# A diffusion layer on one core: neighbourhood attention moved in among the value projection, scores built on 128 rows

## The chip, the core and the metric

The kernel runs on one core of a Trainium2 chip. A core has a matrix engine (PE, whose weight loads are a queue of their own, PEld), a vector engine (DVE), a scalar engine (ACT), a general engine (POOL) and a queue that mostly starts transfers (SP), all with queues of their own that run in order. The metric is the device time of one launch in microseconds (us), as the median of several runs. A profiled execution gives in addition a trace of every instruction.

## The reference

One layer over 256 latent tokens and 256 context tokens of width 2048. All tokens are normalised, modulated and projected by `w_in`. Two branches read the result: a neighbourhood attention with 16 heads of 64, and a gated linear attention (GLA); their outputs are gated, projected and added to the input.

```python
h   = layer_norm(x)   * (1 + scale)   + shift
h_c = layer_norm(ctx) * (1 + scale_c) + shift_c
aq, ak, av, az, bq, bk, bv, bz, bg, mga, mgb = split_cols(h @ w_in)      # and the same of h_c
# attention: each latent query, one softmax over its window of the 4 x 64 grid and all context keys
s   = concat(q * 64**-0.5 @ k_window + bias, q * 64**-0.5 @ k_ctx)
y_a = softmax(s) @ concat(v_window, v_ctx)
y_b = gla(bq, bk, bv, bg, ...)
out = (sigmoid(mga) * ((y_a * silu(az)) @ w_br_a) + sigmoid(mgb) * ((y_b * silu(bz)) @ w_br_b)) @ w_out
x   = layer_norm(2**0.25 * x + gate * out)
```

## The kernel before

The modulated tokens lie transposed in SBUF as a high part `hhi` and a low part `hlo` of reduced-precision floats. A product with a weight block is three matmuls: high by high, low weight by high, high weight by low. Each weight block comes by one SP transfer into a tile `r_...` (pool `raw`, four buffers); ACT casts it to `h_...` and DVE subtracts to get `l_...` (three buffers each).

The program is written as a sequence of stages; a scheduler fixes from it the order of each engine's instructions before the run, and may pull independent work between dependent work.

- Modulation with the key projection of the first seven head pairs (`kp`, copied to `kT`).
- The value projection (`va`): three thirds of 352 columns, in each 8 weight blocks by 4 token tiles by 6 matmuls. At the end of a third the four accumulators are copied to `vs`. The last 32 columns (`lt`, `lp`, `lr`) feed the GLA's gates.
- The attention, one pair of heads `p` after the other (8 pairs). `project_pair(p)` splits the pair's keys into `kn` (high) and `kl` (low), copies the 64 rows of each head into both halves of `kh` by four POOL transfers, and projects the queries (`qp`, 48 matmuls of 256 columns; pair 7 projects its keys, `kp`, too). The queries of head `j` go to `qs`: the high part in the head's 64 rows, the low part in the other 64.
- `attend(p)` takes the 256 queries in two halves `qt`. For both heads there are two matmuls into `s`: `qs` by `kh` over 128 rows (high and low query by high key), and `qs` by `kl` over the head's own 64 rows (high query by low key). DVE adds the bias `rb` and takes the negated maximum `nm`, ACT exponentiates both heads into `pr` and sums into `sm`, DVE inverts `sm` and scales both heads, PE transposes the probabilities in 128x128 blocks (`tp`), ACT copies head 0's to `pt`, DVE head 1's. After both halves the products of values and probabilities follow: 8 calls, each into 64 of the 128 rows of `op`, and a copy to `ya`. Each of these calls is two instructions in the trace, since its operands are full floats.
- `attend(p)` stands behind `project_pair(p + 1)` in the program, so that PE has the next pair's projection to do while a softmax runs. Pair 7's attention runs beside the first GLA projections (`bk`, `bq`).
- The GLA by heads (functions in a list `later` are called at set places in it), the gates and the output projections.

Of the kernel before, what the change touches and what calls it, by code (L numbers as in the profile page):

```python
# [8 lines left out]
F32 = mybir.dt.float32  # L9
F32R = mybir.dt.float32r  # L10
# [6 lines left out]
P = 128  # L17
# [70 lines left out]
def tile_backbone_layer(  # L88
# [251 lines left out]
    for p in range(K0):  # L340
# [3 lines left out]
        else:  # L344
            nc.scalar.copy(dst, kdst[p])

    vs = [k8([P, 2, 1024], f"v{i}") for i in range(2)]
    lr = const.tile([P, 512], F32R, name="lr")
    for g in range(3):
        va = [acc(f"va{g}_{t}") for t in range(4)]  # L350
        for k in range(0, KT, 2):
            wh, wl = load(wav[8 * g + k // 2], 2 * AVW, f"av{g}_{k}")
            project_rows([t[:, :AVW] for t in va], wh, wl, k, AVW, 4)
        n = min(AVW, 1024 - AVW * g)
        for t in range(4):
            dst = vs[t // 2][:, t % 2, AVW * g : AVW * g + n]
            if t % 2:
                nc.vector.tensor_copy(dst, va[t][:, :n])
            else:
                nc.scalar.copy(dst, va[t][:, :n])  # L360
        if g == 2:
# [12 lines left out]
    ya = k8([P, NP, T], "ya")  # L374
    half = [slice(64 * j, 64 * j + 64) for j in range(2)]

    def project_pair(p):
        kT = kTs[p // 4][:, p % 4, :]
        if p >= K0:
            kp = acc(f"kp{p}")  # L380
            project_t(f"ak{p}", kp[:], 512, hhi, hlo)
            nc.scalar.copy(kT, kp[:])
        kn = k2([P, 512], f"kn{p}", F32R)
        kl = k2([P, 512], f"kl{p}", F32R)
        split(kn[:], kl[:], kT)
        kh = k4([P, 2, 512], f"kh{p}", F32R)
        for j in range(2):
            for r in half:
                nc.gpsimd.dma_start(kh[r, j, :], kn[half[j], :])
        qp = acc(f"qp{p}")  # L390
        project_t(f"aq{p}", qp[:, :T], T, xh, xl)
        qs = k2([P, 2, T], f"qs{p}", F32R)
        for j in range(2):
            r, o = half[j], half[1 - j]
            nc.scalar.mul(qs[r, j, :], qp[r, :T], 0.125)
            nc.vector.scalar_tensor_tensor(
                qs[o, j, :], qp[r, :T], 0.125, qs[r, j, :].bitcast(F32), ALU.mult, ALU.subtract
            )
        return qs, kh, kl

    def attend(p, qs, kh, kl):
        rt = stream.tile([P, 1024], F32, tag="raw", name=f"rb{p}", bufs=4)
        nc.sync.dma_start(rt[:, :768], rpb[p])
        rb = rt[:, :768].rearrange("p (j c) -> p j c", j=2)
        pt = k8([P, 2, 4, T], f"pt{p}")
        for qt in range(2):
            s2 = pair(f"s{p}_{qt}")
            for j in range(2):
                q = slice(P * qt, P * qt + P)
                mm(s2[:, j, :], qs[:, j, q], kh[:, j, :], True, False)  # L410
                mm(s2[:, j, :], qs[half[j], j, q], kl[half[j], :], False, True)
            o = P * (1 - qt)
            nc.vector.tensor_tensor(out=s2[:, :, :T], in0=s2[:, :, :T], in1=rb[:, :, o : o + T], op=ALU.add)
            nm = tiny([P, 2], "nm")
            nc.vector.tensor_reduce(nm[:], s2[:], AX.X, ALU.max, negate=True)
            pr = k4([P, 2, 512], f"pr{p}_{qt}")
            sm = tiny([P, 2], "sm")
            for j in range(2):
                nc.scalar.activation(
                    pr[:, j, :], s2[:, j, :], AF.Exp, bias=nm[:, j : j + 1], accum_out=sm[:, j : j + 1]  # L420
                )
            nc.vector.reciprocal(sm[:], sm[:])
            for j in range(2):
                nc.vector.tensor_scalar(pr[:, j, :], pr[:, j, :], sm[:, j : j + 1], None, ALU.mult)
                tp = bank(f"tp{p}_{qt}_{j}")
                for kt in range(4):
                    nc.tensor.transpose(tp[:, P * kt : P * kt + P], pr[:, j, P * kt : P * kt + P], ident[:])
                dst = pt[:, j, :, P * qt : P * qt + P]
                src = tp[:].rearrange("p (k q) -> p k q", k=4)
                if j:  # L430
                    nc.vector.tensor_copy(dst, src)
                else:
                    nc.scalar.copy(dst, src)
        op = bank(f"op{p}")
        for kt in range(4):
            for j in range(2):
                c = 128 * p + 64 * j
                mm(
                    op[64 * j : 64 * j + 64, :T],
                    vs[kt // 2][:, kt % 2, c : c + 64],  # L440
                    pt[:, j, kt, :],
                    kt == 0,
                    kt == 3,
                )
        nc.scalar.copy(ya[:, p, :], op[:, :T])

    ready = project_pair(0)
    for p in range(NP):
        ahead = project_pair(p + 1) if p + 1 < NP else None
        attend(p, *ready)  # L450
        ready = ahead


    cs = const.tile([P, 3, T], F32, name="cs")
# [43 lines left out]
                ALU.mult,  # L498
            )

    later = []

    for h in range(NH):
        zp = pair(f"z{h}")
# [420 lines left out]
```

## Time and profile before

| | us |
|---|---|
| median of 3 runs | 1271.01 (1270.85 to 1273.25) |
| the profiled execution: time / span of its trace | 1274.22 / 1272.5 |
| PE busy in the span | 1236.7 |
| value projection, 139.9 to 232.1 in the trace | 92.2 |
| rest of the attention and first GLA key projections, to the first `bq` at 378.6 | 146.5 |

The span is the trace from its first to its last instruction; the time includes what lies around it. A matmul's bar in the trace overlaps with the next one's, so "PE busy" does not say how fast PE gets on: that is read from the starts of successive matmuls.

### The profile page before, as it was taken

To read this page: it belongs to the slowest core of one execution; us is meant where nothing else is said; L and a number is where in the kernel's file an instruction comes from. 1 tells how busy PE (TensorE), PEld (TensorE's weight loads), DVE (VectorE), ACT (ScalarE), POOL (GpSimd) and SP (SyncE) were. 2 spreads that over 40 slices of the span, in tenths; PEclk is the share of its full clock that TensorE was granted. 3 is DMA by queue.
4 is the path that set the end of the run, shared out by engine and by line. 5 is a ranking of instruction groups with operands and counts; after the bars stand their busy time and mean duration, and the time that the engine had idled before them with its cause. 6 is when DMAs were issued, how large, how long until landed. Compare 5 with 4: busy or idle time off the path is not lost.

```text
span 1272.5 us, 17957 instructions
## 1 busy us (share of the span) xinstructions
PE 1236.7 (97%) x7188; PEld 1053.0 (83%) x7188; DVE 739.7 (58%) x1079; ACT 519.6 (41%) x726; POOL 83.1 (7%) x116
## 2 busy tenths in 40 slices
PE   6999999999999999999999999999999999999994
PEld 4667999976679898898888999998888888888784
DVE  7733322666659457456465477875445554555687
ACT  6333322454445333333342454454444444444341
POOL 1111000110201010010010000000000000000112
PEclk9999999999999999999999999999999999999998
DMA  9997333544524325225234367885656555557651
GB/s 378 417 404 283 90 98 107 156 132 132 146 83 146 125 77 183 85 91 173 95 104 150 113 193 244 281 264 197 198 188 194 190 190 191 191 186 289 206 194 66
DMA packets 61427, 229.94 MB, mean 181 GB/s; under 512 B 7377, under 2 KB 7905, under 8 KB 56225
## 3 DMA queue, kind: packets, MB, share of 16 engines
q1 hardware_dynamic: 53424, 189.83, 45.5%
q0 software_dynamic: 7488, 38.68, 8.1%
q8 instruction: 56, 0.92, 0.3%
q10 hardware_dynamic: 432, 0.30, 0.1%
q14 instruction: 27, 0.21, 0.0%
HBM read 222.49 MB, written 2.10 MB: 176 GB/s over the span
## 4 chain that ended last, share of the span: by engine, by line
PE 85%; DVE 5%; DMA 5%; issue 3%; ACT 1%; POOL 0%; SPq 0%; DVEq 0%; POOLq 0%; ACTq 0%
PE bv L139 14%; PE va L139 7%; PE mgb L139 7%; PE mga L139 7%; PE pb L139 7%; PE bk L139 7%; PE kp L139 6%; PE bz L139 6%; PE qp L139 4%; PE pa L139 3%; PE az L139 3%; PE wo L139 3%; PE gp L139 2%; DMA wm<-in_wmod 2%; PE o L139 2%
## 5 line engine op out<-in xcount | busy, mean ns | idle before, releaser
L139 PE MATMUL bv<-l_bv,hhi 128*128 128x512 f32 x256 | 100.0, 391 | 1.0 <-DVE l_bv L145 1.0
L139 PE MATMUL bv<-h_bv,hhi 128*128 128x512 f32 x256 | 99.7, 389 | 0.0
L139 PE MATMUL bv<-h_bv,hlo 128*128 128x512 f32 x256 | 99.6, 389 | 0.0
L139 PE MATMUL bz<-hhi,l_bz 128*128 128x256 f32 x256 | 72.5, 283 | 1.1 <-DVE l_bz L145 1.1
L139 PE MATMUL bz<-hhi,h_bz 128*128 128x256 f32 x256 | 72.4, 283 | 0.0
L139 PE MATMUL bz<-hlo,h_bz 128*128 128x256 f32 x256 | 72.4, 283 | 0.0
L145 DVE TENSOR_TENSOR l_pb<-r_pb,h_pb 128x1024 fp32r<-128x1024 f32 x32 | 39.2, 1225 | 47.8 <-ACT h_pb L143 47.8
L145 DVE TENSOR_TENSOR l_mgb<-r_mgb,h_mgb 128x1024 fp32r<-128x1024 f32 x32 | 39.2, 1225 | 42.2 <-ACT h_mgb L143 42.2
L139 PE MATMUL va<-h_av,hlo 128*128 128x352 f32 x192 | 62.1, 323 | 0.0
L139 PE MATMUL va<-h_av,hhi 128*128 128x352 f32 x192 | 61.9, 322 | 0.0
L139 PE MATMUL va<-l_av,hhi 128*128 128x352 f32 x192 | 61.7, 322 | 0.0
L145 DVE TENSOR_TENSOR l_mga<-r_mga,h_mga 128x1024 fp32r<-128x1024 f32 x32 | 39.2, 1224 | 35.7 <-ACT h_mga L143 35.6
L482 DVE SCALAR_TENSOR_TENSOR gacc<-wg,sc,gacc 128x1024 f32<-128x1024 f32 x32 | 41.1, 1284 | 30.3 <-DMA wg<-in_wgate 30.3
L139 PEld LDWEIGHTS bv<-l_bv,hhi 128*128 128x128 f32 x256 | 48.1, 188 | 11.7 <-DVE l_bv L145 1.9
L145 DVE TENSOR_TENSOR l_av<-r_av,h_av 128x704 fp32r<-128x704 f32 x24 | 21.4, 892 | 60.4 <-ACT h_av L143 60.4
L139 PEld LDWEIGHTS bv<-h_bv,hlo 128*128 128x128 f32 x256 | 48.1, 188 | 9.9
L139 PEld LDWEIGHTS bv<-h_bv,hhi 128*128 128x128 f32 x256 | 48.1, 188 | 9.8
L143 ACT CAST h_bv<-r_bv 128x1024 fp32r<-128x1024 f32 x32 | 33.5, 1048 | 54.7 <-PE bv L139 49.1
L143 ACT CAST h_mgb<-r_mgb 128x1024 fp32r<-128x1024 f32 x32 | 33.7, 1054 | 53.1 <-PE mgb L139 33.1
L145 DVE TENSOR_TENSOR l_bv<-r_bv,h_bv 128x1024 fp32r<-128x1024 f32 x32 | 39.8, 1251 | 26.2 <-ACT h_bv L143 26.2
L139 PE MATMUL kp<-hhi,h_ak 128*128 128x512 f32 x128 | 52.8, 412 | 0.4 <-ACT hhi L143 0.4
L143 ACT CAST h_mga<-r_mga 128x1024 fp32r<-128x1024 f32 x32 | 33.7, 1054 | 47.1 <-PE mga L139 30.5
(326 smaller groups left out, 3655.0 us busy)
## 6 DMA issues: line engine op xcount, KB each, us to landing
wm<-in_wmod POOLq DMA_DIRECT2D x28, 1024.0 KB, 9.5
r_bv<-in_wst SPq DMA_DIRECT2D x32, 512.0 KB, 3.5
wg<-in_wgate SPq DMA_DIRECT2D x32, 512.0 KB, 4.1
r_bz<-in_wst SPq DMA_DIRECT2D x32, 512.0 KB, 4.5
r_mga<-in_wst SPq DMA_DIRECT2D x32, 512.0 KB, 3.5
r_mgb<-in_wst SPq DMA_DIRECT2D x32, 512.0 KB, 3.5
r_pb<-in_wst SPq DMA_DIRECT2D x32, 512.0 KB, 3.4
r_wo<-in_wst SPq DMA_DIRECT2D x24, 512.0 KB, 4.4
```

What stands on the lines that cost most here:

```text
L139: nc.tensor.matmul(o, a, b, start=start, stop=stop)
L143: nc.scalar.copy(hi, src)
L145: nc.vector.tensor_tensor(out=lo, in0=src, in1=hi.bitcast(F32), op=ALU.subtract)
L482: nc.vector.scalar_tensor_tensor(half, raw[:], sc[:, n // 2, 0:1], half, ALU.mult, ALU.add)
```

## The change

- `value_columns(g)`, one third of the value projection, becomes a function. Four rounds `g` project the pairs 2g and 2g + 1, attend both, and then project a third of the values (in the first three rounds).
- `attend` stops at the transposed probabilities `pt`; the value products are `read_values(p)`. Those of a round's two pairs run in the next round, between its two query projections, once their third of the values is there. Those of pair 6 come at the end of round 3, those of pair 7 are the first entry in `later`.
- Scores on 128 rows: `kh` now holds head `j`'s high keys in 64 rows and its low keys in the other 64; `qh` holds the high queries in both halves, `ql` the low queries in both. Both matmuls of a head contract over 128 rows. The second half of `qh` is one more ACT instruction per head, the second half of `ql` one more POOL transfer per head. (The product of low query and low key, left out before, is now in the sum.)
- Of the two scalings of probabilities in a half, ACT takes head 1's. The value products of head 1 stand ahead of head 0's.

```diff
-        kh = k4([P, 2, 512], f"kh{p}", F32R)
-        for j in range(2):
-            for r in half:
-                nc.gpsimd.dma_start(kh[r, j, :], kn[half[j], :])
...
-            nc.scalar.mul(qs[r, j, :], qp[r, :T], 0.125)
-            nc.vector.scalar_tensor_tensor(
-                qs[o, j, :], qp[r, :T], 0.125, qs[r, j, :].bitcast(F32), ALU.mult, ALU.subtract
-            )
...
-                mm(s2[:, j, :], qs[:, j, q], kh[:, j, :], True, False)
-                mm(s2[:, j, :], qs[half[j], j, q], kl[half[j], :], False, True)
...
-    ready = project_pair(0)
-    for p in range(NP):
-        ahead = project_pair(p + 1) if p + 1 < NP else None
-        attend(p, *ready)
-        ready = ahead
+        for j in range(2):
+            for r, src in zip(half, (kn, kl)):
+                nc.gpsimd.dma_start(kh[r, j, :], src[half[j], :])
...
+            nc.scalar.mul(qh[r, j, :], qp[r, :T], 0.125)
+            nc.vector.scalar_tensor_tensor(
+                ql[r, j, :], qp[r, :T], 0.125, qh[r, j, :].bitcast(F32), ALU.mult, ALU.subtract
+            )
+            nc.scalar.mul(qh[o, j, :], qp[r, :T], 0.125)
+            nc.gpsimd.dma_start(ql[o, j, :], ql[r, j, :])
...
+                mm(s2[:, j, :], qh[:, j, q], kh[:, j, :], True, False)
+                mm(s2[:, j, :], ql[:, j, q], kh[:, j, :], False, True)
...
+                if j:
+                    nc.scalar.mul(pr[:, j, :], pr[:, j, :], sm[:, j : j + 1])
+                else:
+                    nc.vector.tensor_scalar(pr[:, j, :], pr[:, j, :], sm[:, j : j + 1], None, ALU.mult)
...
+    def read_values(p):
+        pt = probs.pop(p)
+        op = bank(f"op{p}")
+        for kt in range(4):
+            for j in (1, 0):
+                c = 128 * p + 64 * j
+                mm(op[64 * j : 64 * j + 64, :T], vs[kt // 2][:, kt % 2, c : c + 64], pt[:, j, kt, :], kt == 0, kt == 3)
+        nc.scalar.copy(ya[:, p, :], op[:, :T])
...
+    for g in range(4):
+        q = k8([P, 2, 2, 2, T], f"q{g}", F32R)
+        pairs[2 * g] = project_pair(2 * g, q)
+        for p in sorted(probs):
+            read_values(p)
+        if g == 3:
+            probs[6] = attend(6, *pairs.pop(6))
+        pairs[2 * g + 1] = project_pair(2 * g + 1, q)
+        for p in sorted(pairs):
+            probs[p] = attend(p, *pairs.pop(p))
+        if g < 3:
+            value_columns(g)
+    read_values(6)
...
-    later = []
+    later = [lambda: read_values(NP - 1)]
```

On PE, the scores of pair 0's second half of queries (`s0_1`) stood before like this, with two of the next pairs' query projections around them; `x4` is a run of four equal rows:

```order
L139 MATMUL qp2_2293<-hhi_89,h_aq2_8_2326 128x256
L139 MATMUL s0_1_2247<-kh0_2071,qs0_2137 128x512
L139 MATMUL s0_1_2247<-kl0_2068,qs0_2137 128x512
L139 MATMUL s0_1_2247<-kh0_2071,qs0_2137 128x512
L427 MATMUL tp0_0_0_2234<-ident_73,pr0_0_2228 128x128 x4
L427 MATMUL tp0_0_1_2241<-ident_73,pr0_0_2228 128x128 x4
L139 MATMUL s0_1_2247<-kl0_2068,qs0_2137 128x512
L139 MATMUL qp2_2293<-hhi_89,l_aq2_8_2327 128x256
L139 MATMUL qp2_2293<-hlo_90,h_aq2_8_2326 128x256
```

Now the same scores stand among the values' first third, and no row reads `kl`. An `x3` here is three of the four score matmuls:

```order
L139 MATMUL va0_0_1566<-h_av0_2_1602,hlo_90 128x352
L139 MATMUL s0_1_1482<-kh0_1300,q0_1295 128x512 x3
L405 MATMUL tp0_0_0_1469<-ident_73,pr0_0_1463 128x128 x4
L139 MATMUL s0_1_1482<-kh0_1300,q0_1295 128x512
L405 MATMUL tp0_0_1_1476<-ident_73,pr0_0_1463 128x128 x4
L139 MATMUL va0_1_1567<-h_av0_2_1602,hhi_89 128x352
```

What moved: the four score matmuls are of one kind, and the work that covers the softmax is `va` instead of `qp`.

The value products of pair 0 (`op0`; `64x256` is the shape written) stood before in two pieces, with eight matmuls of a query projection in between, of which the first and the last are shown:

```order
L139 MATMUL s1_0_2362<-kl1_2143,qs1_2212 128x512
L139 MATMUL op0_2274<-pt0_2219,v0_1291 64x256
L139 MATMUL qp3_2435<-hlo_90,h_aq3_0_2438 128x256
...
L139 MATMUL qp3_2435<-hhi_89,h_aq3_8_2468 128x256
L139 MATMUL op0_2274<-pt0_2219,v0_1291 64x256 x3
L139 MATMUL op0_2274<-pt0_2219,v1_1292 64x256 x4
L139 MATMUL qp3_2435<-hhi_89,l_aq3_8_2469 128x256
```

Now the products of pairs 0 and 1 stand in one piece between two query projections:

```order
L139 MATMUL qp2_1824<-hlo_90,h_aq2_8_1857 128x256
L139 MATMUL op0_1893<-pt0_1454,v0_1292 64x256 x4
L139 MATMUL op0_1893<-pt0_1454,v1_1293 64x256 x4
L139 MATMUL op1_1903<-pt1_1511,v0_1292 64x256 x4
L139 MATMUL op1_1903<-pt1_1511,v1_1293 64x256 x4
L139 MATMUL qp3_1922<-hhi_89,h_aq3_0_1925 128x256
```

What moved: sixteen calls run back to back, and the first of them comes behind `qp2`, after the whole first third of the values.

On POOL there were four transfers per pair, issued together; these are the last two pairs' and what follows them, up to the GLA's tiles `gacc` and `wr`:

```order
L389 DMA kh6_2856<-kn6_2852 64x512 x4
L389 DMA kh7_3060<-kn7_3056 64x512 x4
L475 MEMSET gacc_3278 128x2048
L476 DMA gacc_3278<-in_bgate 1x16x128
L461 DMA wr_3267<-in_wg2 128x1024
```

Now a round has eight for `kh` and four that bring the other half of `ql` (a part of tile `q`; `q3` is round 3's). This is the same place:

```order
L362 DMA kh6_2925<-kn6_2921 64x512
L362 DMA kh6_2925<-kl6_2922 64x512
L362 DMA kh6_2925<-kn6_2921 64x512
L362 DMA kh6_2925<-kl6_2922 64x512
L373 DMA q3_2920<-q3_2920 64x256 x2
L362 DMA kh7_3142<-kn7_3138 64x512 x2
L362 DMA kh7_3142<-kl7_3139 64x512 x2
L373 DMA q3_2920<-q3_2920 64x256 x2
L493 MEMSET gacc_3296 128x2048
L494 DMA gacc_3296<-in_bgate 1x16x128
L479 DMA wr_3285<-in_wg2 128x1024
```

What moved: a pair's scores now wait for two short POOL transfers that can start only behind its query projection. In round 3, on PE, pair 6's scores stand behind the value products of pairs 4 and 5; pair 7's first score matmul stands behind eight rows of `bk00`, the next two behind six more, the last behind eight more.

## Rows read from the trace of the kernel before

**Rows 1.** The page: the span, and from its first part PE's busy time, share of the span and instructions.

```profile
span 1272.5 us, 17957 instructions
PE 1236.7 (97%) x7188; PEld 1053.0 (83%) x7188; DVE 739.7 (58%) x1079; ACT 519.6 (41%) x726; POOL 83.1 (7%) x116
```

**Rows 2.** Busy time by stage: from the first value matmul to the last, and from there to the first `bq`. Columns: stretch and its length, then busy time and instructions of PE, PEld, DVE, ACT and POOL, PE's granted clock as a share of 2.4 GHz, share of the 16 transfer engines, GB/s.

```profile
139.90:232.10 92.20, 92.20 (x578) 92.14 (x576) 25.67 (x34) 22.48 (x32) 0.00 (x0) 1.00 0.35 103
232.10:378.60 146.50, 144.16 (x853) 109.24 (x852) 98.08 (x157) 68.99 (x136) 17.11 (x31) 0.99 0.46 134
```

**Rows 3.** PE in order of time, the score matmuls of one half of a pair and what stands around them. Columns: start, duration, engine, line, written <- read, shapes, count. What an instruction costs PE is the time to the next start.

```profile
249.43 0.39 PE L139 MATMUL s<-kh,qs 128*128 128x512 f32 x1
249.76 0.49 PE L139 MATMUL s<-kl,qs 64*128 64x512 f32 x1
250.18 0.50 PE L139 MATMUL s<-kh,qs 128*128 128x512 f32 x1
250.51 1.04 PE L427 MATMUL tp<-ident,pr 128*128 128x128 f32 x8
251.48 0.50 PE L139 MATMUL s<-kl,qs 64*128 64x512 f32 x1
251.91 0.38 PE L139 MATMUL qp<-hhi,l_aq 128*128 128x256 f32 x1
252.13 0.28 PE L139 MATMUL qp<-hlo,h_aq 128*128 128x256 f32 x1
```

**Rows 4.** PE in order of time, undisturbed stretches: second and last of the 48 matmuls of one query projection (256 columns), and second and last of 22 matmuls of a key projection (512 columns).

```profile
268.65 0.28 PE L139 MATMUL qp<-hhi,h_aq 128*128 128x256 f32 x1
274.15 0.28 PE L139 MATMUL qp<-hhi,l_aq 128*128 128x256 f32 x1
...
337.63 0.40 PE L139 MATMUL bk<-hhi,h_bk 128*128 128x512 f32 x1
342.21 0.39 PE L139 MATMUL bk<-hlo,h_bk 128*128 128x512 f32 x1
```

**Rows 5.** PE in order of time: eight transposes between matmuls of a projection.

```profile
373.68 1.03 PE L427 MATMUL tp<-ident,pr 128*128 128x128 f32 x8
374.47 0.48 PE L139 MATMUL bk<-hhi,l_bk 128*128 128x512 f32 x1
```

**Rows 6.** PE in order of time: pair 0's value products, a piece of two and a piece of fourteen instructions, with the matmuls next to them.

```profile
259.26 0.65 PE L139 MATMUL op<-pt,v 128*64 128x256 f32 x2
259.84 0.39 PE L139 MATMUL qp<-hlo,h_aq 128*128 128x256 f32 x1
260.06 0.28 PE L139 MATMUL qp<-hhi,h_aq 128*128 128x256 f32 x1
...
260.77 0.28 PE L139 MATMUL qp<-hhi,h_aq 128*128 128x256 f32 x1
260.98 1.94 PE L139 MATMUL op<-pt,v 128*64 128x256 f32 x14
262.85 0.39 PE L139 MATMUL qp<-hhi,l_aq 128*128 128x256 f32 x1
```

**Rows 7.** Waits around pair 4's value products: PE in order of time (the brackets give idle time and who ended it), PE's clock in the stretch behind the wait (columns as in rows 2), and ACT's cast that came late.

```profile
308.45 0.40 PE L139 MATMUL kp<-hhi,h_ak 128*128 128x512 f32 x1
310.37 0.65 PE L139 MATMUL op<-pt,v 128*64 128x256 f32 x2 [1.52 <-ACT pt L433]
311.52 3.42 PE L139 MATMUL op<-pt,v 128*64 128x256 f32 x14
314.87 0.50 PE L139 MATMUL kp<-hlo,h_ak 128*128 128x512 f32 x1
...
327.90 0.49 PE L139 MATMUL s<-kl,qs 64*128 64x512 f32 x1
329.10 0.65 PE L139 MATMUL op<-pt,v 128*64 128x256 f32 x2 [0.71 <-ACT pt L433]
...
311.00:314.50 3.50, 3.50 (x15) 1.83 (x15) 1.10 (x1) 0.00 (x0) 0.00 (x0) 0.52 0.38 112
...
308.66 1.04 ACT L143 CAST h_aq<-r_aq 128x1024 fp32r<-128x1024 f32 x1 [1.88 <-DMA r_aq<-in_wst]
```

**Rows 8.** DVE and ACT in order of time, one softmax: the bias is added, the last exponential begins to be summed (the next score matmul may start behind it).

```profile
268.90 0.69 DVE L413 TENSOR_TENSOR s<-s,rb 128x512 f32<-128x512 f32 x1
270.10 1.22 DVE L415 TENSOR_REDUCE nm<-s 128x2 f32<-128x1024 f32 x1
...
272.60 0.20 ACT L419 ACTIVATION_READ_ACCUMULATOR pr<-s,nm 128x1 f32 x1
```

**Rows 9.** Groups of instructions between 232 and 378 us (columns: line, engine, operation, names, shapes, count, busy us, mean ns), then POOL's own share of a transfer (min, median, max ns), and from issue to landing: the 32 transfers of 128 KB to `kh` (us, min, median, max), and one of 4 KB near 109 us (count, KB, us).

```profile
L395 ACT ACTIVATE qs<-qp 64x256 fp32r<-64x256 f32 x16 | 6.1, 378 | 7.4 <-PE qp L139 5.9 <-PE s L139 1.4
L396 DVE SCALAR_TENSOR_TENSOR qs<-qp,qs 64x256 fp32r<-64x256 f32 x16 | 6.8, 422 | 1.5 <-ACT qs L395 0.9
L145 DVE TENSOR_TENSOR l_aq<-r_aq,h_aq 128x1024 fp32r<-128x1024 f32 x14 | 17.1, 1224 | 9.1 <-ACT h_aq L143 8.9
...
L389 POOL DMA_DIRECT2D kh<-kn x32: 509/519/544, 137.6 to 338.1; - x32
DMA to landing us min/median/max: 2.2/4.6/7.4
...
bgt<-in_bg POOLq DMA_DIRECT2D x1, 4.0 KB, 9.3
```

More of the change, by code (lines that the diff above doesn't have):

```diff
@@ L345, in tile_backbone_layer, with project_pair @@
             nc.scalar.copy(dst, kdst[p])
+    ya = k8([P, NP, T], "ya")
+    half = [slice(64 * j, 64 * j + 64) for j in range(2)]
+    def project_pair(p, q):
+        kT = kTs[p // 4][:, p % 4, :]
+        if p >= K0:
+            kp = acc(f"kp{p}")
+            project_t(f"ak{p}", kp[:], 512, hhi, hlo)
+            nc.scalar.copy(kT, kp[:])
+        kn = k2([P, 512], f"kn{p}", F32R)
+        kl = k2([P, 512], f"kl{p}", F32R)
+        split(kn[:], kl[:], kT)
+        kh = k4([P, 2, 512], f"kh{p}", F32R)
+        for j in range(2):
+            for r, src in zip(half, (kn, kl)):
+                nc.gpsimd.dma_start(kh[r, j, :], src[half[j], :])
+        qp = acc(f"qp{p}")
+        project_t(f"aq{p}", qp[:, :T], T, xh, xl)
+        qh, ql = q[:, p % 2, 0], q[:, p % 2, 1]
+        for j in range(2):
+            r, o = half[j], half[1 - j]
+            nc.scalar.mul(qh[r, j, :], qp[r, :T], 0.125)
[4 more added lines that the diff above has]
+            nc.gpsimd.dma_start(ql[o, j, :], ql[r, j, :])
+        return qh, ql, kh
@@ new lines, in attend @@
+    def attend(p, qh, ql, kh):
+        rt = stream.tile([P, 1024], F32, tag="raw", name=f"rb{p}", bufs=4)
+        nc.sync.dma_start(rt[:, :768], rpb[p])
+        rb = rt[:, :768].rearrange("p (j c) -> p j c", j=2)
+        pt = k8([P, 2, 4, T], f"pt{p}")
+        for qt in range(2):
+            s2 = pair(f"s{p}_{qt}")
+            for j in range(2):
+                q = slice(P * qt, P * qt + P)
+                mm(s2[:, j, :], qh[:, j, q], kh[:, j, :], True, False)
+                mm(s2[:, j, :], ql[:, j, q], kh[:, j, :], False, True)
+            o = P * (1 - qt)
+            nc.vector.tensor_tensor(out=s2[:, :, :T], in0=s2[:, :, :T], in1=rb[:, :, o : o + T], op=ALU.add)
+            nm = tiny([P, 2], "nm")
+            nc.vector.tensor_reduce(nm[:], s2[:], AX.X, ALU.max, negate=True)
+            pr = k4([P, 2, 512], f"pr{p}_{qt}")
+            sm = tiny([P, 2], "sm")
+            for j in range(2):
+                nc.scalar.activation(
+                    pr[:, j, :], s2[:, j, :], AF.Exp, bias=nm[:, j : j + 1], accum_out=sm[:, j : j + 1]
+                )
+            nc.vector.reciprocal(sm[:], sm[:])
+            for j in range(2):
+                if j:
+                    nc.scalar.mul(pr[:, j, :], pr[:, j, :], sm[:, j : j + 1])
+                else:
+                    nc.vector.tensor_scalar(pr[:, j, :], pr[:, j, :], sm[:, j : j + 1], None, ALU.mult)
+                tp = bank(f"tp{p}_{qt}_{j}")
+                for kt in range(4):
+                    nc.tensor.transpose(tp[:, P * kt : P * kt + P], pr[:, j, P * kt : P * kt + P], ident[:])
+                dst = pt[:, j, :, P * qt : P * qt + P]
+                src = tp[:].rearrange("p (k q) -> p k q", k=4)
+                if j:
+                    nc.vector.tensor_copy(dst, src)
+                else:
+                    nc.scalar.copy(dst, src)
+        return pt
@@ L347, in tile_backbone_layer @@
+    def read_values(p):
+        pt = probs.pop(p)
+        op = bank(f"op{p}")
+        for kt in range(4):
+            for j in (1, 0):
+                c = 128 * p + 64 * j
+                mm(
+                    op[64 * j : 64 * j + 64, :T],
+                    vs[kt // 2][:, kt % 2, c : c + 64],
+                    pt[:, j, kt, :],
+                    kt == 0,
+                    kt == 3,
+                )
+        nc.scalar.copy(ya[:, p, :], op[:, :T])
     vs = [k8([P, 2, 1024], f"v{i}") for i in range(2)]
@@ L348, in tile_backbone_layer, with value_columns @@
     lr = const.tile([P, 512], F32R, name="lr")
-    for g in range(3):
+    def value_columns(g):
         va = [acc(f"va{g}_{t}") for t in range(4)]
@@ L372, in tile_backbone_layer @@
                 nc.vector.tensor_tensor(out=lr[r, :], in0=lp[r, :], in1=lr[r, :].bitcast(F32), op=ALU.subtract)
[L374 to L385, printed above, removed]
-        kh = k4([P, 2, 512], f"kh{p}", F32R)
-        for j in range(2):
-            for r in half:
-                nc.gpsimd.dma_start(kh[r, j, :], kn[half[j], :])
[L390 to L394, printed above, removed]
-            nc.scalar.mul(qs[r, j, :], qp[r, :T], 0.125)
-            nc.vector.scalar_tensor_tensor(
-                qs[o, j, :], qp[r, :T], 0.125, qs[r, j, :].bitcast(F32), ALU.mult, ALU.subtract
-            )
-        return qs, kh, kl
@@ L401, in attend @@
[L401 to L409, printed above, removed]
-                mm(s2[:, j, :], qs[:, j, q], kh[:, j, :], True, False)
-                mm(s2[:, j, :], qs[half[j], j, q], kl[half[j], :], False, True)
[L412 to L445, printed above, removed]
@@ L447, in tile_backbone_layer @@
-    ready = project_pair(0)
-    for p in range(NP):
-        ahead = project_pair(p + 1) if p + 1 < NP else None
-        attend(p, *ready)
-        ready = ahead
+    probs, pairs = {}, {}
+    for g in range(4):
[10 more added lines that the diff above has]
+            value_columns(g)
```

## The prediction

> **What bounds the kernel now.** I read the page's busy times first. PE, the matrix engine, is busy 97% of the span, 1236.7 of 1272.5 us, and no other engine comes near [rows 1]. So the time is the sum of what PE's queue costs, plus its few waits. The change touches the stretch from the first value matmul to the first `bq`, so I read the windows next: 92.2 us of values and 146.5 us behind them, 238.7 us together [rows 2]. After the change the same products lie in one stretch of the same two ends.
>
> A bar of PE overlaps the next, so I then read PE in order of time and took the distance from start to start as what an instruction costs. Undisturbed rates: a value matmul 92.2/576 = 0.160 us [rows 2]; a query-projection matmul (268.65 to 274.15, 46 steps) 0.1196 us; one of 512 columns (337.63 to 342.21, 20 steps) 0.229 us [rows 4]; a transpose, eight in 0.79 us, 0.099 us [rows 5].
>
> The places that cost more than their rate are the attention's. In a score group the `kh` matmuls last 0.33 us to the next start, and the `kl` matmuls over 64 rows 0.42 and 0.43 us, although both have 512 columns; the projection matmul behind takes 0.22 instead of 0.12 [rows 3]. A piece of value products costs 0.58 us for two instructions and 1.87 us for fourteen, so 1.29/12 = 0.1075 us for each further one and 0.58 - 2 x 0.1075 = 0.37 us for coming and going; the projection matmul next to it loses another 0.10 behind and some 0.09 ahead. I call that 0.56 us per piece [rows 6]. Last come the waits: before pair 4's value products PE stands 1.7 us beyond a matmul's step (308.45 to 310.37), its clock falls to 0.52 of 2.4 GHz, so to its lower level, and the next fourteen instructions take 3.35 us instead of 1.87; further on 0.8 us are lost [rows 7]. That wait ends with a copy of ACT whose queue stood behind a late weight transfer [rows 7].
>
> **The sum without new waits.** Work that stays: 576 value matmuls 92.2 us, 384 of query projections 45.9 us, 144 of `kp7`, `bk00` and `bk01` 33.0 us, four of `lp` 0.4 us: 171.5 us. Before, 238.7 - 171.5 = 67.2 us are left for scores, transposes, value products, their switches and waits. After: 64 scores, all over 128 rows, at 0.229 us: 14.7; 128 transposes at 0.099: 12.7; 128 instructions of value products at 0.1075: 13.8; four blocks of them with 0.56 us each: 2.2. Together 43.4 us, so **23.8 us less**.
>
> The same by parts: a score group cost 249.43 to 251.91 plus 0.10 behind, 2.58 us, and should cost 4 x 0.229 + 0.79 = 1.71 us, which over 16 halves saves 13.9 us. Twelve of sixteen pieces of value products go, 6.7 us (each pair has two pieces now). The waits of before go too, 4.0 us, since value products read probabilities made a round earlier. Sum 24.6, which agrees.
>
> What no row of before shows is a low-query score over 128 rows. It reads full operands like `kh`'s. Its bounds are 0.229 us (the projection with the same 512 columns) and 0.43 us (the old `kl` row). I take 0.229: within a group the two kinds alternate, `kh`'s also lost 0.10 there although its rows are full, so the loss sits at the change between 64 and 128 rows, and there is none any more. Here I weigh the Trainium skill. "TensorE: Matmul & The Clock Gate", section "Why this matters for your kernels", says that a matmul over few rows takes as long as one over 128 and that only concurrent tiles gain; by it alone filling the rows gives nothing, which is the first rival below. "TensorEngine Tiling (Array Packing)", section "Key Properties", says against it that a change of tiling mode drains the engine; by that the whole difference goes. The 0.33 and 0.42 us side by side agree with the second.
>
> **New waits (a): the second half of `ql`.** It comes by a POOL transfer that can start only behind the query projection. ACT's multiplication takes 0.38, DVE's subtraction 0.42 [rows 9], and I add 0.2 for the steps between: head 0's half arrives 1.0 + L behind the projection, with L the time from issue to landing. Head 1's comes 2.2 us later: a weight split of 1.22 on DVE in between, its own 0.42, POOL's 0.52 for one issue [rows 9]. On PE, the scores that need them follow so, at the rates above: `s0` after the 48 matmuls of `qp1`, at 6.0 us (head 0) and 6.4 (head 1); `s2` and `s4` after two pairs' value products and a projection, 9.8 and 10.3; `s6` after pairs 4 and 5's value products, 4.0, head 1's after five `kp7` matmuls more, 5.6; `s7` after eight, then six `bk00`, 3.4 and 5.7. The odd pairs of the first rounds come behind a whole attention.
>
> L is not in the trace. Nearest are `kh`'s transfers, 2.2 to 7.4 us with a median of 4.6, four of 128 KB at once; a 4 KB one took 9.3 us elsewhere [rows 9]. These are 64 KB, two at a time. I take 3.7, between the least and the median. Then `s0` waits 6.9 - 6.4 = 0.5 us, `s6` 1.3, `s7` 1.2: 3.0 us. With L = 2.2 nothing waits; with 6.2 it is 3.0 + 3.8 + 3.7 = 10.5 us.
>
> The Trainium skill, "DMA: Bandwidth & Descriptors", section "Anatomy of one DMA — SWDGE (gpsimd) path", gives 2.0 us plus the bytes at 436 GB/s. For 64 KB that is an estimate of 2.15 us; by it these waits vanish and the median would be 1249.7 us. The rows, with two thirds of their landings far above, decide for the longer time.
>
> **(b) The softmax.** From the addition of the bias to the end of the last exponential, which frees the score bank for the next half, it takes 268.90 to 272.80, 3.9 us [rows 8]. Its cover is now 24 to 30 value matmuls, 3.84 to 4.8 us. Weight casts and splits of the values stand in the same queues, some 0.7 us each (22.48/32 on ACT, 25.67/34 on DVE [rows 2]). Bounds: nothing, if none stands in front; 12 halves x (3.9 + 0.7 - 3.84) = 9 us, if one always does on the shortest cover. I take 2.
>
> **(c) The clock.** The waits above are short; the one fall in the stretch followed 1.5 us of idle time and cost 1.5 us [rows 7]. Bounds 0 and three falls, 4.5 us; I take 0.5.
>
> **Costed at nothing.** ACT gets 16 multiplications (6.1 us by rows 9's mean) and 16 scalings (at most 0.69 each, the bias addition's time [rows 8]), 17 us; with 91.5 us in the stretch before [rows 2] it is then busy half the time, as is DVE, which gives its scalings up. Value matmuls of PE hide that; without cover each scaling adds up to 0.69 us to the path to `pt`, which is now read a round later. Weight blocks come through the same four buffers while the transfer engines are 35 to 46% busy [rows 2]; a bias tile holds one of them for a whole attention, and a late block would show as a cast that waits, as in rows 7. POOL has 16 issues more, 8 us, beside 17 us of work in 146 [rows 2]. The transfers to `kh` now wait for the low part too, one DVE subtraction later; they are needed a whole query projection afterwards, 5.7 us.
>
> **The sum.** 23.8 - 3.0 - 2.0 - 0.5 = 18.3 us. The profiled execution took 1274.2 us, 0.25% above the median of 1271.0, so 1255.9 on its scale and **1253 us** as a median.
>
> **The rivals.**
> - *128 rows cost no less.* If the 0.42 of the `kl` rows belongs to a change of operands and not of rows, the 13.9 us stay. For it: `kh` too takes 0.33, with 128 rows. Against it: projections change operands at each step and take 0.229. Gain 4.4 us, 1266.6 us. 8%.
> - *The `ql` halves land late*, at L = 6.2, near the top of `kh`'s range: 10.5 us of waits, three clock falls 4.5, softmax 2, gain 6.8 us, **1264 us**. For it: landings of 7.4 in this stretch, beside weight blocks on the same transfer engines. Against it: half the size, half the number. 15%.
> - *The other side: landings like the 9.3 us one.* Head 1's half then comes 12.5 us behind the projection: `s0` 6.1, `s2` and `s4` 2.2 each, `s6` 6.9, `s7` 6.8, 24.2 us; clock falls 5 and softmax 2 give 31, a loss of 7.4 us: **1278 us**. It decides from where waits pass 23.8 - 7 = 16.8 us, 10.5 + 3(L - 6.2) + 2(L - 7.1), so from L of 7.8 on. For it: one such row. Against it: none of 32 landings here passed 7.4. 6%.
> - *Nothing comes of it*: the casts stand in each softmax's way (9 us) and half of the landings are late, the gain is eaten to within a few us. 3%.
>
> **How the numbers follow.** The forecast has 68%; its own range is 1247 (no waits at all, 23.8 us) to 1262 (waits of 9 us in the softmax, 5 of transfers). The first two rivals reach 1267 and I take the range to 1264, 1247 to 1264, which leaves out half of the first two rivals and the last two. About 0.2% is what a measurement of this kernel tells from no change. Faster by more: the forecast and the first two rivals, less their bad tails, 0.88; within it 0.05; slower 0.07.
>
> **What would show it.** In the changed kernel: score matmuls 0.23 us from start to start, none over 64 rows; four blocks of 32 value-product instructions at 0.1075 each; from the first query projection to the first `bq` about 220 us; the waits, if any, ahead of the first scores of pairs 0, 6 and 7, ended by a POOL transfer; no wait ahead of `op`. Wrong would be: score rows of 0.33 or more; waits of PE for the exponentials in the value stretches; the granted clock below 1.00 in many slices; weight casts that wait for their transfer, which would say that the four buffers don't suffice.

## The result, and the profile after

The changed kernel's median is 1263.95 us (four runs, 1261.88 to 1265.59) against 1272.13 us of the kernel before beside it. That is the median of four runs, one of which took 4339.79 us; without it, it is 1271.01 us. The ratio is 0.993, 95% interval 0.9918 to 0.9942, so 0.7% faster: some 9 us by the ratio, 7 by the medians without that run. The forecast was 18.3 us less, 1253 us. The sign was right and the time lies in the range, but the gain is less than half of the one forecast.

The page of the profiled execution, 1261.88 us; the answer to [rows 1]:

```profile
span 1260.2 us, 18039 instructions
PE 1221.6 (97%) x7188; PEld 1052.3 (84%) x7188; DVE 735.3 (58%) x1063; ACT 535.4 (42%) x758; POOL 90.7 (7%) x132
```

PE is still the bound, with exactly as many instructions; its bars add up to 15 us less. The four rounds by time, from the first query projection to the first `bq` (columns as in [rows 2]):

```profile
140.16:190.69 50.53, 50.26 (x338) 48.01 (x336) 29.73 (x43) 27.59 (x53) 8.51 (x17) 1.00 0.60 159
190.69:244.56 53.87, 53.85 (x371) 50.40 (x370) 27.71 (x39) 24.99 (x48) 6.12 (x12) 1.00 0.46 133
244.56:298.42 53.86, 53.84 (x370) 50.40 (x370) 27.46 (x42) 24.93 (x48) 4.07 (x8) 1.00 0.43 122
298.42:365.57 67.15, 63.19 (x359) 50.52 (x358) 35.14 (x56) 32.01 (x55) 7.67 (x12) 0.97 0.39 119
```

Together 225.41 us, against 238.7 before and 220.4 forecast. In the middle rounds PE never waits, ACT and DVE are half busy as reckoned, and yet a round is 53.87 us where the sum's terms give 53.0: 30.7 of values, 11.5 of two projections, 4.0 of value products, 6.8 of scores and transposes. In the last round PE waits 4 us and its mean clock is 0.97. These are the two places to read.

First, PE in order of time in round 0, the place of [rows 3]:

```profile
157.71 0.32 PE L139 MATMUL va<-h_av,hlo 128*128 128x352 f32 x1
158.06 0.96 PE L139 MATMUL s<-kh,q 128*128 128x512 f32 x3
158.87 0.60 PE L405 MATMUL tp<-ident,pr 128*128 128x128 f32 x4
159.22 0.48 PE L139 MATMUL s<-kh,q 128*128 128x512 f32 x1
159.54 0.60 PE L405 MATMUL tp<-ident,pr 128*128 128x128 f32 x4
159.89 0.41 PE L139 MATMUL va<-h_av,hhi 128*128 128x352 f32 x1
160.14 0.33 PE L139 MATMUL va<-l_av,hhi 128*128 128x352 f32 x1
```

Three scores take 0.81 us and the fourth, behind transposes, 0.32. The group is 1.83 us (2.48 before), not 1.71. Its neighbours lose too: the value matmul behind takes 0.25 and the one ahead 0.35 instead of 0.16. Second, the value products, the answer to [rows 6]:

```profile
196.32 0.28 PE L139 MATMUL qp<-hlo,h_aq 128*128 128x256 f32 x1
196.53 3.67 PE L139 MATMUL op<-pt,v 128*64 128x256 f32 x32
200.14 0.39 PE L139 MATMUL qp<-hhi,h_aq 128*128 128x256 f32 x1
200.36 0.28 PE L139 MATMUL qp<-hhi,l_aq 128*128 128x256 f32 x1
```

From 196.53 to 200.14, 3.61 us for 32 instructions, with 0.09 and 0.10 at the neighbours 3.8 us; 4.0 were forecast. Third, the waits of the last round, in order of time (brackets: idle time and who ended it), the clock behind the second, and POOL's issues ahead of it:

```profile
308.29 0.50 PE L139 MATMUL s<-kh,q 128*128 128x512 f32 x1
310.04 0.70 PE L139 MATMUL s<-kh,q 128*128 128x512 f32 x2 [1.25 <-DMA q<-q]
...
332.64 0.39 PE L139 MATMUL bk<-hhi,l_bk 128*128 128x512 f32 x1
335.40 0.47 PE L139 MATMUL s<-kh,q 128*128 128x512 f32 x1 [2.37 <-DMA kh<-kl]
...
336.60:340.30 3.70, 3.70 (x11) 2.70 (x10) 0.00 (x0) 0.00 (x0) 1.34 (x3) 0.54 0.42 134
...
327.82 1.02 POOL L362 DMA_DIRECT2D kh<-kn  x2 [19.20 <-ACT kn L143]
329.16 1.02 POOL L362 DMA_DIRECT2D kh<-kl  x2 [0.33 <-DVE kl L145]
332.35 0.51 POOL L373 DMA_DIRECT2D q<-q  x1 [2.17 <-DVE q L369]
```

And from issue to landing: the first transfer of low keys here (count, KB, us), and all sixteen of `ql` (us).

```profile
kh<-kl POOLq DMA_DIRECT2D x1, 128.0 KB, 6.1
...
DMA to landing us min/median/max: 1.9/2.6/4.8
```

Pair 6 waits 1.25 us for its `ql` half, as forecast (1.3). Pair 7 does not wait for `ql` first but for `kh`'s low keys, issued at 329.16, and 2.37 us of idle time are followed by 3.7 us at 0.54 of the clock. That wait was costed at nothing.

### The profile page after: what moved, and what is told of

Same layout as the page of the kernel before. It is cut to its first block, busy times and chain, and to the rows that moved or that the text cites. A ratio compares the mean times of both kernels' runs of the same rounds, so it can differ in the third digit from the quotient of the medians.

```text
span 1260.2 us, 18039 instructions
## 1 busy us (share of the span) xinstructions
PE 1221.6 (97%) x7188; PEld 1052.3 (84%) x7188; DVE 735.3 (58%) x1063; ACT 535.4 (42%) x758; POOL 90.7 (7%) x132
## 4 chain that ended last, share of the span: by engine, by line
PE 83%; DVE 6%; issue 5%; DMA 3%; ACT 2%; POOL 0%; DVEq 0%; SPq 0%; POOLq 0%; ACTq 0%
PE bv L139 14%; PE kp L139 7%; PE mgb L139 7%; PE mga L139 7%; PE pb L139 7%; PE bz L139 6%; PE bk L139 6%; PE va L139 6%; PE pa L139 3%; PE qp L139 3%; PE az L139 3%; PE wo L139 3%; PE gp L139 2%; PE o L139 2%; PE s L139 1%
## 5 line engine op out<-in xcount | busy, mean ns | idle before, releaser
L145 DVE TENSOR_TENSOR l_pb<-r_pb,h_pb 128x1024 fp32r<-128x1024 f32 x32 | 39.2, 1225 | 47.8 <-ACT h_pb L143 47.8
L145 DVE TENSOR_TENSOR l_mgb<-r_mgb,h_mgb 128x1024 fp32r<-128x1024 f32 x32 | 39.2, 1225 | 42.1 <-ACT h_mgb L143 42.1
L145 DVE TENSOR_TENSOR l_mga<-r_mga,h_mga 128x1024 fp32r<-128x1024 f32 x32 | 39.2, 1225 | 35.8 <-ACT h_mga L143 35.7
L145 DVE TENSOR_TENSOR l_bv<-r_bv,h_bv 128x1024 fp32r<-128x1024 f32 x32 | 38.8, 1220 | 29.8 <-ACT h_bv L143 29.8
L143 ACT CAST h_pb<-r_pb 128x1024 fp32r<-128x1024 f32 x32 | 33.7, 1053 | 43.4 <-PE pb L139 30.1
```

Of the source, the lines that this page charges most:

```text
L143: nc.scalar.copy(hi, src)
L145: nc.vector.tensor_tensor(out=lo, in0=src, in1=hi.bitcast(F32), op=ALU.subtract)
```

## The experiments

**The two kernels once more.** They stand first because a sum made on one profiled execution rests on that execution.

> The kernel before, unchanged, once more. Theory A (the base of the sum was wrong): the 4.0 us around pair 4's value products (1.7 us of waiting for the copy of pt behind a late weight block, 1.5 us at the lower clock, 0.8 us) were a chance of the execution that was profiled, so other executions have less of them: the median lies near 1271, and a profile of such an execution shows the stretch from the first value matmul to the first bq 2 to 4 us shorter than 238.7, with no PE wait above 1 us in it. Rival B: these waits are in every execution, the stretch is 238.7 again, and the 3 us between the profiled time and the median lie elsewhere.

Measured: 1272.24 us, ratio 1.0004 (0.9995 to 1.0013). The profile took 1271.78 us, and the stretch was 236.44 us (140.76 to 377.20), 2.3 us shorter than 238.7. PE around pair 4's value products, the place of [rows 7] (its other wait there, 0.7 us in [rows 7], is 0.6 here):

```profile
310.63 0.65 PE L139 MATMUL op<-pt,v 128*64 128x256 f32 x2 [0.35 <-ACT pt L433]
311.21 0.50 PE L139 MATMUL kp<-hhi,l_ak 128*128 128x512 f32 x1
...
311.64 1.94 PE L139 MATMUL op<-pt,v 128*64 128x256 f32 x14
313.51 0.50 PE L139 MATMUL kp<-hlo,h_ak 128*128 128x512 f32 x1
```

The same wait is 0.35 us here, and the fourteen instructions take 1.87 us, not 3.35: no clock fall. So theory A holds, and 2.3 of the 4.0 us that I had counted as saved were not there to be saved in this execution.

> The changed kernel, unchanged, once more. Its four runs went from 1261.9 to 1265.6, and the profiled one was the fastest. Theory A: what differs between executions is when transfers land ahead of the scores of pairs 6 and 7, so the waits there (1.25 and 2.37 us before) change from one profile to the next by 1 to 3 us and with them the half-clock stretch behind them; a median of 1263 to 1265. Rival B: these waits are the same to within 0.3 us each time and executions differ in the first 140 us or behind 366 us.

Measured: 1261.92 us (six runs, 1259.35 to 1264.2), 0.9927 (0.9913 to 0.9941); the median is below the 1263 to 1265 expected. The profile took 1260.45. The stretch was 223.67 us, and these are PE's waits in it and just behind it, where the one ahead of `bq` lies (columns: who waited for what, us in total, times, longest):

```profile
PE s L139 <- DMA kh<-kl: 2.0, 1, 2.0
PE s L139 <- DMA q<-q: 1.8, 3, 1.0
PE bq L139 <- DVE l_bq L145: 0.6, 1, 0.6
```

The waits stand at the same places, and the clock did not fall behind 2.0 us of idle time (granted 1.00 from 334.2 to 342) where it had behind 2.37; the score and `bk` matmuls take 1.7 us less for it, which is the 1.7 us between the two profiles. The waits themselves moved by 0.3 to 0.4 us, less than theory A said.

**The rows of the scores, taken back.** In the changed kernel:

```
-  kh[r, j, :] <- (kn, kl)[half[j]]       # two halves
+  kh[r, j, :] <- kn[half[j]]             # as before
-  mm(s2[:, j], qh[:, j, q], kh[:, j]);  mm(s2[:, j], ql[:, j, q], kh[:, j])
+  mm(s2[:, j], qs[:, j, q], kh[:, j]);  mm(s2[:, j], qs[half[j], j, q], kl[half[j]])
```

> The changed kernel with the scores as before: kl over 64 rows, four transfers to kh from kn, no second half of ql; the new order of the attention, values in blocks and the scaling on ACT stay. Theory (64-row rows cost 0.42 us, and a change of rows around them): per half of queries 0.5 to 0.87 us more on PE, 8 to 14 us in all, less 2.3 us of waits for ql and up to 2.4 us for kh: 1268 to 1275 us, and score rows of 0.33 and 0.42 us between value matmuls. Rival (128 rows cost no less): the same or up to 4 us faster than the changed kernel, 1260 to 1264.

Measured: 1265.34 us, 0.9955 (0.9943 to 0.9967), so 3.4 us slower than the changed kernel on the same chip, less than the theory's least. The stretch was 230.56 us, 5.2 and 6.9 more than in the two profiles of the changed kernel. PE in order of time:

```profile
159.18 0.50 PE L139 MATMUL s<-kh,q 128*128 128x512 f32 x1
159.61 0.50 PE L139 MATMUL s<-kl,q 64*128 64x512 f32 x1
160.04 0.50 PE L139 MATMUL s<-kh,q 128*128 128x512 f32 x1
160.39 0.60 PE L403 MATMUL tp<-ident,pr 128*128 128x128 f32 x4
160.91 0.50 PE L139 MATMUL s<-kl,q 64*128 64x512 f32 x1
161.35 0.66 PE L403 MATMUL tp<-ident,pr 128*128 128x128 f32 x4
161.76 0.40 PE L139 MATMUL va<-l_av,hhi 128*128 128x352 f32 x1
```

PE waits once in the stretch, ahead of pair 7's scores:

```profile
PE s L139 <- DMA kh<-kn: 1.1, 1, 1.1
```

A group takes 2.58 us here and 1.83 in the changed kernel. So full rows do save: scores and transposes together, from each row's start to the next, take 39.2 us of this stretch and 29.8 in the second profile of the changed kernel, 9.4 us less, 0.6 a group. Waits take 2.7 us of it back (1.1 us here, 3.8 there), since the 128-row scores also bring the transfers of `ql` and the later `kh`; that leaves the 6.9 us of the two stretches. The medians show only 3.4; the profiled execution here was the slowest of six, 2.0 us above the median, and the other 1.5 us below its own. Pair 7 waits for `kh` with high keys alone, too, and in no run of the old order does PE wait for `kh`: the wait comes with the new order, and the later low keys make it longer. The other side of the same run: order, blocks and scaling without new scores gain 6.0 us over the kernel before.

**The same part alone, in the old order.**

```
 project_pair, attend: as in the change (kh with low keys, qh, ql, POOL transfer)
 loop over pairs, value products, scalings: as before
```

> The kernel before with one part of the change alone: scores on 128 rows, kh with low keys in its other half, qh and ql with the POOL transfer; order, value products and scalings as before. Theory (the 128-row scores save, but not the switches between scores and transposes, 0.09 to 0.11 us each): score groups of 1.8 to 1.95 us in place of 2.48 and 0.10, 16 x 0.65 = 10 us less, and with the projection of the next pair between, hardly a wait for ql: 1260 to 1263 us. By my forecast's working (no switch): 13.9 us less, 1257. Rival (rows cost the same): 1270 to 1272 us or, with waits for ql, more.

Measured: 1279.4 us, 1.005 (1.0032 to 1.0068): slower than before, and neither theory had it. The score groups cost what they should (0.23 us a matmul in a row): scores and transposes take 8.9 us less of the stretch than in the second profile of the kernel before, so the saving is there in the old order too. But the stretch is 243.9 us against 236.4. PE waits 11.8 us, where it had waited 1.3, 8.9 us of it ahead of value products and 2.9 once for `ql`, which was expected to cost hardly a wait; projections of queries and value products, in part at the lower clock behind such waits, take 6.0 us more. ACT in order of time, PE where it waits, and the sums of the waits:

```profile
276.73 0.20 ACT L422 ACTIVATION_READ_ACCUMULATOR pr<-s,nm 128x1 f32 x1
279.97 1.04 ACT L143 CAST h_aq<-r_aq 128x1024 fp32r<-128x1024 f32 x1 [3.04 <-DMA r_aq<-in_wst]
280.92 0.58 ACT L436 COPY pt<-tp 128x512 f32<-128x512 f32 x1
...
281.55 0.65 PE L139 MATMUL op<-pt,v 128*64 128x256 f32 x2 [2.22 <-ACT pt L436]
283.51 3.32 PE L139 MATMUL op<-pt,v 128*64 128x256 f32 x14
...
ACT h_aq L143 <- DMA r_aq<-in_wst: 10.4, 6, 3.0
PE op L139 <- ACT pt L436: 8.9, 4, 2.3
PE s L139 <- DMA ql<-ql: 2.9, 1, 2.9
```

A weight cast waits 3.04 us for its transfer, the copy that PE needs stands behind it in ACT's queue, and the fourteen instructions then take 3.25 us (granted clock 0.59 from 283.5 to 287). It is the chain of [rows 7]; PE waits so four times. Why the weights came late was tried twice.

```
-  rt = raw tile;  sync.dma_start(rt[:, :768], rpb[p])
+  rb = kTs[1][:, :2, :T]                 # run one: no tile
+  rt = raw tile;  gpsimd.memset(rt[:, :768], 0)   # run two: the tile, no transfer
```

> The kernel before with 128-row scores alone, and without the bias tile rb: what is added to the scores is read from the key tile, so the output lacks the bias, and no transfer of rb takes one of the four raw buffers. Theory (128-row scores in the old order make the attention outrun its weights: casts of r_aq waited 1.5 to 3.0 us for their transfer while a bias tile held a buffer, the copies to pt stood behind them in ACT's queue, and PE lost 8.9 us ahead of op): the casts' waits and PE's waits ahead of op fall to under 3 us, 1262 to 1268 us against 1279 with the tile. Rival (the late copies come from ACT's own extra work or the POOL transfers): the waits ahead of op stay above 6 us and the time above 1274.

> The kernel before with 128-row scores alone, and the bias tile still in a raw buffer, but filled with zeros by POOL in place of its transfer of 384 KB (so the bias is left out). It tells the buffer from the bytes. Theory (the tile holds one of four buffers through an attention, so weight transfers start late): casts of r_aq wait again and PE waits 5 to 9 us ahead of op, 1273 to 1279 us. Rival (the bytes: 384 KB more per pair on the transfer engines and the SP queue): as without the tile, 1266 to 1269 us.

Measured: 1267.36 us without the tile (0.9966, 0.9954 to 0.9978), and neither does a cast of `r_aq` wait for a transfer nor PE ahead of a value product; the stretch is 229.0 us, 7.4 less than in the second profile of the kernel before. It is 1275.31 us with the tile and without its bytes (1.0025, 1.0012 to 1.0039), and there the waits are:

```profile
ACT h_aq L143 <- DMA r_aq<-in_wst: 8.9, 5, 2.6
PE op L139 <- ACT pt L436: 7.4, 4, 2.3
```

So most of it is the buffer: a bias tile holds one of four through an attention, and in the old order a shorter attention outruns the weights. The bytes or SP's issue may hold the remaining 3 to 4 us; the intervals of the runs with and without the bytes overlap, and it was not taken further. PE's one wait for `ql` is there in all three runs (2.9 us with the tile, 1.3 without, 3.4 with the tile of zeros), so the transfers cost something in the old order as well. In the changed kernel casts wait 1.5 and 2.2 us in its two profiles, and PE never for them. The order is thus what lets the 128-row scores pay.

**The POOL transfers.**

```
-  nc.gpsimd.dma_start(ql[o, j, :], ql[r, j, :])
+  nc.vector.scalar_tensor_tensor(ql[o, j, :], qp[r, :T], 0.125, qh[r, j, :], mult, subtract)
```

> The changed kernel, with the second half of ql written by one more DVE instruction per head (0.42 us, 16 in all) in place of the POOL transfer. Theory (the late ql halves cost what the waits show): the waits ahead of the scores of pairs 0 and 6 (0.2 to 0.3 and 1.0 to 1.5 us) go, the one ahead of pair 7 stays, since it ends with a transfer to kh: 1.5 to 2 us less than the changed kernel, 1260 us. Rival (DVE pays for it: its weight splits come later and PE waits for those): within 0.5 us of the changed kernel or slower, waits of PE for l_aq or l_av.

Measured: 1257.63 us, 0.99 (0.9884 to 0.9916): 4.3 us less than the changed kernel by the medians, 3.4 by the ratios, whose intervals overlap. In the profile the stretch is 221.95 us, 1.7 us shorter than in the second profile of the changed kernel, as expected: 1.8 us of waits for `ql` are gone and 1.0 of pair 7's for `kh`, while value matmuls wait 0.7 us and a transpose 0.3 us for DVE. The medians moved more than that. Behind the first `bq` this profile has 893.8 us where that of the changed kernel had 895.4; besides, the changed kernel's executions vary by 4.9 us, and the two that were profiled are among its faster ones.

```
 for pair 7, in place of split and four transfers:
+  nc.scalar.copy(kh[r, j, :], kT[r])
+  nc.vector.tensor_tensor(kh[o, j, :], kT[r], kh[r, j, :], subtract)
```

> As the run with ql by DVE, and in addition pair 7's kh written by two ACT casts and two DVE subtractions in place of cast, subtraction and four POOL transfers. Theory (pair 7's wait of 2.0 to 2.4 us is the landing of its low keys, 6.1 us behind the issue): that wait and the half-clock stretch that sometimes follows it go too: 4 to 6 us less than the changed kernel, 1256 to 1258 us, no PE wait over 0.5 us from the first query projection to the first bq. Rival (something else is late there as well, weight blocks of bk00 or the queries): a wait of 1 us or more stays ahead of pair 7's scores and the gain is under 3 us.

Measured: 1255.97 us (four runs, 1255.79 to 1256.96), 0.9879 (0.9866 to 0.9892), 6.0 us less than the changed kernel and 1.2% faster than before. PE's waits in the stretch of 220.99 us:

```profile
PE va L139 <- DVE q L380: 0.7, 3, 0.3
PE tp L414 <- DVE pr L411: 0.3, 1, 0.3
```

The theory holds in this: nothing else was late behind pair 7's keys. The price of DVE's extra instruction is 0.7 us. But in the stretch the gain on the second profile of the changed kernel is 2.7 us, the waits alone; most of the rest of the 6.0 us would be behind the first `bq`, where this profile has 892.5 us and that one 895.4.

**The scaling on ACT**, taken back:

> The changed kernel with both scalings on DVE, as before. Theory (costed at nothing): within 1 us of the changed kernel, 1261 to 1263.5 us. Rival (the shorter chain from scores to transposes is part of the gain): PE waits in the value stretches, 2 to 8 us slower.

Measured: 1262.29 us, 0.9929 (0.9916 to 0.9942), the changed kernel's own ratio. It was rightly costed at nothing: no gain and no loss can be told.

**The order of scores and transposes.** On the kernel in which ACT and DVE write `ql` and pair 7's `kh`, which is called the one without POOL transfers (those to `kh` of pairs 0 to 6 remain):

```
+  with tc.issue_after(last score matmul of the second half):
       transposes of the first half
```

> As the run without POOL transfers, and the transposes of a pair's first half are put behind the last score matmul of its second half, so that four scores and eight transposes follow each other with one change between them. Theory (each change between scores, transposes and the projection costs 0.08 to 0.11 us on PE, and my sum had none): groups of 0.93 + 0.8 us with 0.1 on the matmul behind, in half of the groups one or two changes fewer, 1 to 1.5 us less than without POOL transfers: 1254.5 to 1255.5 us. Rival (the order of PE's rows doesn't matter, slots are 0.31 where records end late): no difference in the stretch, 1256.

Measured: 1255.55 us (1254.42 to 1257.82), 0.9872 (0.9858 to 0.9885). The stretch is 221.03 us against 220.99. PE in order of time:

```profile
212.01 1.11 PE L139 MATMUL s<-kh,q 128*128 128x512 f32 x4
212.95 1.03 PE L397 MATMUL tp<-ident,pr 128*128 128x128 f32 x8
213.74 0.40 PE L139 MATMUL va<-l_av,hhi 128*128 128x352 f32 x1
213.99 0.32 PE L139 MATMUL va<-h_av,hlo 128*128 128x352 f32 x1
```

The group is 1.73 us, which is the sum's 1.71, but the value matmul behind takes 0.25 in place of 0.16, and other matmuls lose what the groups gain: over the stretch scores and transposes take 0.8 us less than in the run without POOL transfers, the other matmuls 1.1 us more, and waits 0.3 us less. The theory's 1 to 1.5 us fell; why the others lose was not tried.

## Why the prediction was right in sign and wrong in size

First the stretch by kinds of matmul, from the second profile of each kernel. A row is charged with the time to the next row's start, waits taken off.

| us | before | changed | the prediction's sum |
|---|---|---|---|
| values, query and key projections, `lp` (what stays) | 175.8 | 175.1 | 171.5 |
| two rows `z` of the GLA, before behind the first `bq` | 0 | 0.6 | 0 |
| scores | 24.7 | 17.3 | 14.7 |
| transposes | 15.1 | 12.5 | 12.7 |
| value products | 19.6 | 14.4 | 16.0 |
| PE's waits; in the sum (a), (b) and (c) | 1.3 | 3.8 | 5.5 |
| the stretch | 236.4 | 223.7 | 220.4 |

By the prediction's own steps, with what the runs put in their place:

- *PE sets the time, the slots are the price.* Right. No other engine became the bound, and the order works as described: no PE wait for an exponential or for a copy of `pt` in any of the value stretches.
- *Low-query scores over 128 rows at 0.229 us.* Right: four in a row take 0.94 us. The first rival is out, for the old scores in the new order cost 0.6 us a group more. "TensorE: Matmul & The Clock Gate" of the Trainium skill, whose section "Why this matters for your kernels" has few rows cost as much as many, speaks of a single matmul, and no run here times 64-row ones by themselves. Between 128-row ones the rows with `kl` took 0.42 to 0.44 us in two orders, and the `kh` rows beside them, over 128, 0.33 to 0.43 as well: the loss goes with the alternation, as the prediction argued.
- *The sum without new waits, 23.8 us.* **This step failed, by 5.0 us.** It priced the work that stays as if undisturbed, 171.5 us, and so put the other 67.2 us of the stretch down to what was to change. But this work costs 175 to 176 us in either order, since it loses time at its edges to whatever stands between; neither order gains that part. Scores, too, cost more than their rate where they stand behind transposes, 17.3 us in place of 14.7; value products cost less, 14.4 in place of 16.0. In all PE's matmuls take 219.9 us and the sum had 214.9. It was in sight in [rows 3, 5]: a `kh` score behind other work at 0.33 us, a `bk` matmul behind eight transposes at 0.48 us bar. A middle round, in which PE never waits, shows it alone: 53.87 us where the terms gave 53.0, though its value products were 0.2 us cheaper than reckoned.
- *The waits of before go, 4.0 us.* **This step failed, by 2.3 us.** They were real in the profiled execution, but for the most part not in the next one. Setting the sum against the profiled time and then moving the result by the 0.25% between that execution and the median kept them in. The excess of 3.2 us over the median was a sign that waits of that size in the profile might be its own.
- *(a) The transfers, 3.0 us, with 0.5 for the clock.* The landing of `ql` was taken as 3.7 us: it was 1.9 to 4.8, median 2.6; in the last round, which decides, 3.7 to 4.8 (1.8 to 4.6 in the second profile). By "DMA: Bandwidth & Descriptors" of the Trainium skill, section "Anatomy of one DMA — SWDGE (gpsimd) path", it would have been an estimate of 2.15 us each time; the quiet rounds come near it (2.4 to 2.6), the last does not. What failed is a sentence among the things **costed at nothing**: pair 7's transfers to `kh` were to have 5.7 us of cover, although [rows 9] have landings of these transfers of up to 7.4 us. And the low keys were issued 1.34 us behind the high ones and landed 6.1 us after that, 7.4 us behind the first issue, and PE waited 2.0 to 2.4 us and once lost about 1.6 us more at the lower clock.
- *(b) The softmax, 2 us.* Nothing of it came: 24 value matmuls cover it even with casts in the queue.
- *The scaling on ACT, the weights.* Right: the run on the scaling shows no difference, and no PE wait for a weight block stands in the stretch.

So 18.3 - 2.3 - 5.0 + 1.7 (3.8 us of waits in place of 5.5) is 12.7 us, and the stretch is 12.8 us shorter, 236.44 to 223.67. In the first profiles it is 13.3 us shorter: no 2.3 to take off there, but 6.5 us more on matmuls, 1.6 of them at the lower clock, and waits of 4.1. That the waits came near their allowance was luck: 2 us had been put on the softmax, where nothing came, and nothing on pair 7's keys, where 2.0 to 2.4 came. Luck, too, is that the time equals the second rival's 1264 us: that rival had 10.5 us of waits for `ql` and three falls of the clock, and there were 1.5 to 1.8 us and at most one.

The medians gained less than the stretch, 9.4 us against the 20 runs of the kernel before beside the second run of the changed one. Part of it lies behind the first `bq`, where the changed kernel is 2.5 us longer in the second profiles (895.4 against 892.9 us) and 0.8 in the first. The first 96 `bq` matmuls take 12.39 us there in place of 11.95 (before with the two rows `z` among them), with a wait of 0.6 us for a weight split; the rest is open. The profiles of the new order with `ql` transfers have 894.5 to 895.4 us behind the first `bq`, those without 892.5 to 893.8; why, no run shows.

## What to carry to other kernels

Before a wait in a trace is booked as a gain, look for it in a second execution; the distance of the profiled time from the median says how much may be chance. Work that stays is not free of what is to be moved: taken off at undisturbed rates, it leaves its losses at the edges to the part that changes, and these losses are then forecast as gains. Some 0.1 us at a change between kinds of matmul adds up: here the work that stays and the scores cost 6.2 us more than their rates. And what is costed at nothing because "it is needed much later" deserves the subtraction with the slowest landing in the trace, for the last instance, where the cover is shortest; here short transfers between partitions were better written by the engine that made the data.

## What was not expected of the hardware

- The four transfers of a pair's `kh`, issued within 2.4 us on one queue, landed after 2.3 us for the first and about 6 us for the last ones. The small ones of `ql` took from 1.8 to 4.8 us.
- The first matmul behind transposes costs 0.08 to 0.1 us more, scores and values alike, and putting transposes together did not change the stretch (221.03 and 220.99 us).
- The granted clock fell to 0.54, the lower level, behind 2.37 us of idle time in one execution, and not behind 2.0 and 2.24 us at the same place in two others (the second changed run and the one with both scalings on DVE). In the kernel before it had fallen behind 1.52 us [rows 7], so the length of one wait does not decide it.
- Gains of parts don't add up: new order alone 6.0 us, 128-row scores alone 8 us slower by the medians, both together 9.4 us faster.
